# First feed-forward of a two-stream trunk layer: hidden products written to DRAM, then w2 as seven block products; x is read a second time

## The chip, the cores and the metric

The kernel runs on one core of one Trainium2 chip. The metric is device time in microseconds of one execution, the median of three runs. TensorE (PE) multiplies a stationary 128x128 block by up to 512 moving columns into PSUM; VectorE (DVE), ScalarE (ACT) and GpSimd (POOL) work elementwise; SyncE (SP) issues the transfers between DRAM and SBUF, in the order of its queue.

## The reference

One layer, 1024 latent tokens x and 256 context tokens, width 1024, hidden width 2816. Cut to what matters here:

```python
m_l = split(silu(c) @ ada_w + ada_b, 9)          # modulation, latents
m_c = split(silu(c_ctx) @ ada_w + ada_b, 9)      # modulation, context
x   = x   + 0.5 * m_l[2] * swiglu(modulate(rms_norm(x,   norm1_w), m_l[0], m_l[1]), w1, w3, w2)
ctx = ctx + 0.5 * m_c[2] * swiglu(modulate(rms_norm(ctx, norm1_w), m_c[0], m_c[1]), w1, w3, w2)
y   = token_mixing(modulate(rms_norm(x, norm2_w), m_l[3], m_l[4]),
                   modulate(rms_norm(ctx, norm2_w), m_c[3], m_c[4]), ...)
x   = x + m_l[5] * y
x   = x + 0.5 * m_l[8] * swiglu(modulate(rms_norm(x, norm3_w), m_l[6], m_l[7]), w1', w3', w2')
return rms_norm(x, final_norm_w)
# swiglu(h, w1, w3, w2) = (silu(h @ w1) * (h @ w3)) @ w2
```

## The kernel before

Everything is kept transposed: x is eight tiles (k) of 128 channels by 512 tokens for each of two latent token groups (tg 0 and 1), and eight of 128x256 for the context (tg 2). Each float32 operand is split into a high and a low part (`split`, L56: ScalarE copies the high part, VectorE or GpSimd subtracts for the low part), and one 128x128 block product is three matmuls (`mm3`, L61). The hidden width is 22 blocks f of 128, worked off in eleven pairs.

**Stage 1, first feed-forward of the latents.** `first1` (L632) and two calls of `classic` (L582) do three pairs plainly: for each block and each of w1 and w3, eight k for both token groups. From pair 3 on `sevens` (L599) multiplies the 2x2 arrangement (two halves of k by two token groups, two blocks f) with seven block products instead of eight (`seven`, L276; its weight sums in `seven_w`, L256). The sums of the activations T1 to T4 are made once ahead of it (`t12`, `t34_raw`, `t3_split`, `t4_split`, L493 to L526). In all pairs the product silu(h w1) * (h w3) stays in SBUF (`s3`, L545), and one pair later `Y` (L552) multiplies it plainly by w2 and adds it, gated, into x. So x stays in SBUF through the stage.

**Modulation.** Sixteen columns (shift and scale of the first norm) come early, in `first1`. 32 more latent columns follow at low priority in the plain pairs (`mod_col`, L100: a 512 KB load and a VectorE reduction over 1024 elements, into a ring of seven tiles). The context's 40 columns and 24 latent ones are made half by half during `sevens` (`mods_half`, L112: 256 KB loads through the ring `raw` that the weights use, MLATE = 17 per pair).

**Stage 2, context.** The context's x is loaded and normed, the last pair's `Y` of token group 1 runs, then `classic` and `Y` for the 256 context tokens, pair by pair; GpSimd makes the low parts of w1 and w3 there. The norm of group 1 is handed out over these pairs. Last come `Y` of the last pair for the context and for group 0, the norm of group 0, and a copy of x to DRAM (`xd`).

**Stage 3** is token mixing. **Stage 4**, the second feed-forward, is already in two phases: `hidden` (L397) makes all eleven pairs, nearly all with `chain` (L307, the seven products with accumulation in PSUM), and `g_out` (L357) writes seven activation sums of each pair to DRAM (`gd`). `w2_sums` (L375) writes four sums of w2's blocks per pair (`sd`). Then `back` (L404) does w2 as seven products, each over all eleven pairs, with `pair` loading one activation tile and one weight tile of 256 KB. Its last product also carries the final norm.

**Order.** Instructions are placed by a scheduler by priority: `high_priority(offset=WPRI)` moves weight loads and splits ahead, a negative offset moves work back. Each engine, and SP's queue, then runs its instructions in the fixed order. Rings that matter: `raw` 6 tiles, split weights 6, scratch `s` 7 tiles in the first feed-forward (NS) and 20 in the second.

## Time and profile before

| | us |
|---|---|
| three runs | 2242.12, 2242.82, 2245.99 |
| median | 2242.82 |
| the profiled execution's own time | 2242.13 |
| its span, first to last instruction | 2240.4 |

Roughly, by the windows view: the latents' first feed-forward runs to 720 us, the context to 950, mixing to 1570, the second feed-forward to the end. Of the kernel's 316.47 MB of transfers, 314.39 go through SP's queue.

How to read the rows. A row of a group has line, engine, operation, output <- input, shape and count, then busy time and the mean of one in ns, then the idle time of the engine just before, with what ended it. A row of windows has a stretch in us and, for each engine, busy us with the number of instructions in parentheses, then TensorE's granted clock, the busy share of the transfer engines and their GB/s. A row of waits has who waited for whom, the sum in us, how often, and the longest. A row of the timeline has start, duration, engine, line, operation. A row of one line's instructions has min/median/max of the duration in ns. SPq and POOLq are the queues of SyncE and GpSimd.

### The profile page before, as it was taken

What the parts mean: (1) busy time and instruction counts of PE and PEld (TensorE: products, weight loads), DVE (VectorE), ACT (ScalarE), POOL (GpSimd) and SP (SyncE); (2) the same over time, 40 slices, a digit from 0 to 9 for tenths busy, and PEclk for the clock granted to TensorE, in tenths of its full rate; (3) what the DMA queues carried; (4) which work ended last, traced back from release to release, by engine and by line L of the source; (5) the groups of instructions that cost most, each with busy time, mean ns of one, the idle gap of its engine ahead of it and who ended that gap; (6) DMA issues with size and microseconds to landing.
All of it is one profiled execution on the core that took longest, in us unless ns stands there. A gap on an engine that the chain in (4) does not pass through costs nothing. (4 is left out here: it accounts for less than half of the span.)

```text
span 2240.4 us, 32584 instructions
## 1 busy us (share of the span) xinstructions
PE 2148.4 (96%) x11598; PEld 1829.7 (82%) x11598; DVE 1590.9 (71%) x2901; ACT 919.1 (41%) x1681; POOL 291.4 (13%) x294
## 2 busy tenths in 40 slices
PE   4999999999999999999998999999999999999998
PEld 3888888888887999888877888778778888888888
DVE  7798888888888745763567446867776767675666
ACT  3323223232334554555653445334334343444553
POOL 2000000000002565431032112300000000010000
PEclk9999999999999999999999999999999999999999
DMA  7661444444434566463322223324135445467664
GB/s 246 215 234 40 123 136 137 132 132 136 132 104 136 152 184 186 151 179 107 100 66 73 78 77 88 103 74 164 59 123 166 165 149 170 145 202 239 200 198 151
DMA packets 175859, 316.47 MB, mean 141 GB/s; under 512 B 20880, under 2 KB 34128, under 8 KB 175696
## 3 DMA queue, kind: packets, MB, share of 16 engines
q1 hardware_dynamic: 175696, 314.39, 44.6%
q8 instruction: 91, 1.49, 0.3%
q14 instruction: 72, 0.59, 0.1%
HBM read 260.01 MB, written 45.91 MB: 137 GB/s over the span
## 5 line engine op out<-in xcount | busy, mean ns | idle before, releaser
L58 ACT ACTIVATE whi<-raw 128x512 fp32r<-128x512 f32 (+1 forms) x662 | 408.2, 623 | 805.3 <-PE psa L64 244.0
L59 DVE TENSOR_TENSOR wlo<-raw,whi 128x512 fp32r<-128x512 f32 (+1 forms) x544 | 377.5, 697 | 309.7 <-ACT whi L58 305.9
L63 PE MATMUL psa<-hh,whi 128*128 128x512 f32 (+1 forms) x1460 | 537.0, 369 | 7.7 <-ACT hh L195 7.7
L64 PE MATMUL psa<-hl,whi 128*128 128x512 f32 (+1 forms) x1460 | 537.8, 368 | 2.0 <-DVE hl L196 2.0
L65 PE MATMUL psa<-hh,wlo 128*128 128x512 f32 (+1 forms) x1460 | 537.1, 368 | 0.0
L63 PEld LDWEIGHTS psa<-hh,whi 128*128 128x128 f32 x1460 | 277.3, 190 | 50.9 <-ACT hh L195 9.1
L64 PEld LDWEIGHTS psa<-hl,whi 128*128 128x128 f32 x1460 | 277.8, 190 | 45.2 <-DVE hl L196 3.0
L65 PEld LDWEIGHTS psa<-hh,wlo 128*128 128x128 f32 x1460 | 277.7, 190 | 42.2
L59 POOL TENSOR_TENSOR wlo<-raw,whi 128x512 fp32r<-128x512 f32 (+1 forms) x118 | 158.9, 1362 | 760.5 <-ACT whi L58 753.4
L63 PE MATMUL psb<-ghi,whi 128*128 128x512 f32 (+1 forms) x528 | 188.2, 357 | 3.5 <-ACT ghi L58 2.1
L64 PE MATMUL psb<-glo,whi 128*128 128x512 f32 (+1 forms) x528 | 187.7, 356 | 0.7 <-DVE glo L59 0.6
L65 PE MATMUL psb<-ghi,wlo 128*128 128x512 f32 (+1 forms) x528 | 187.5, 355 | 0.0
L63 PE MATMUL psb<-hh,whi 128*128 128x512 f32 (+1 forms) x420 | 158.6, 380 | 2.3 <-ACT hh L195 1.8
L64 PE MATMUL psb<-hl,whi 128*128 128x512 f32 (+1 forms) x420 | 159.4, 379 | 1.5 <-DVE hl L196 1.5
L65 PE MATMUL psb<-hh,wlo 128*128 128x512 f32 (+1 forms) x420 | 159.1, 379 | 0.6 <-DVE wlo L59 0.6
L561 DVE SCALAR_TENSOR_TENSOR x<-psb,modl,x 128x512 f32<-128x512 f32 x176 | 128.6, 745 | 5.1 <-PE psb L65 4.9
L63 PEld LDWEIGHTS psb<-ghi,whi 128*128 128x128 f32 x528 | 100.2, 190 | 20.3 <-DVE x L561 2.8
L64 PEld LDWEIGHTS psb<-glo,whi 128*128 128x128 f32 x528 | 100.4, 190 | 14.5 <-DVE glo L59 1.1
L65 PEld LDWEIGHTS psb<-ghi,wlo 128*128 128x128 f32 x528 | 100.5, 190 | 13.7
L64 PE MATMUL psa<-wlo,hh 128*128 128x256 f32 (+1 forms) x320 | 94.7, 296 | 0.9 <-DVE wlo L59 0.9
L63 PE MATMUL psa<-whi,hh 128*128 128x256 f32 (+1 forms) x320 | 94.4, 295 | 0.2 <-ACT s L891 0.2
L63 PEld LDWEIGHTS psb<-hh,whi 128*128 128x128 f32 x420 | 79.6, 190 | 17.6 <-ACT hh L195 2.2
(370 smaller groups left out, 3750.1 us busy)
## 6 DMA issues: line engine op xcount, KB each, us to landing
raw<-in_w SPq DMA_DIRECT2D x385, 256.0 KB, 3.0
raw<-in_adaT SPq DMA_DIRECT2D x128, 256.0 KB, 3.2
gd<-s SPq DMA_DIRECT2D x77, 256.0 KB, 2.8
raw<-gd SPq DMA_DIRECT2D x77, 256.0 KB, 2.7
ada<-in_adaT SPq DMA_DIRECT2D x29, 512.0 KB, 4.7
s<-in_w SPq DMA_DIRECT2D x44, 256.0 KB, 4.8
sd<-s SPq DMA_DIRECT2D x44, 256.0 KB, 2.5
raw<-sd SPq DMA_DIRECT2D x44, 256.0 KB, 2.7
```

Source lines behind the costliest of these rows:

```text
L58: nc.scalar.activation(hi, src, AF.Copy)
L59: (eng or nc.vector).tensor_tensor(out=lo, in0=src, in1=hi.bitcast(F32), op=ALU.subtract)
L63: mm(ps, wa[0], xa[0], start=start, stop=False, skip_group_check=more)
L64: mm(ps, wa[0], xa[1], start=False, stop=False, skip_group_check=more)
L65: mm(ps, wa[1], xa[0], start=False, stop=stop, skip_group_check=more)
L561: nc.vector.scalar_tensor_tensor(out=x, in0=ps[:, :n], scalar=self.gates_m[int(tg == 2)][:, m:m + 1], in1=x, op0=ALU.mult, op1=ALU.add)
```

## The change

In the first feed-forward, `first1` and one further plain pair (`classic_g`) are followed by `hidden(4, ...)`, nine pairs of chains whose products go to DRAM; three modulation columns follow each chain. x's tiles are given up after the first norm and read again behind the hidden stage. `back` is taken apart into methods that both feed-forwards use: `back6` does six of the seven products. In the first feed-forward the seventh (product 4) runs behind the context, into PSUM tiles of its own. Only two of w2's four sums are stored (`sd` has two planes); the other two are made from two loads each when products 7 and 3 need them, through a ring of eight tiles (`raw2`) in the place of activations no longer needed. The context's norm runs inside `back6`, behind product 2, at an offset of -300 for its matmuls. Latent modulation columns of the groups 5, 7, 6 and 8 are made half by half in the context loop, six per pair. Columns that latents and context both need share one load. The scratch ring of the first feed-forward has 19 tiles.

```diff
-        self.gd = self.nc.dram_tensor("gd", (8, NP, P, 512), F32, kind="Internal").ap()
-        self.sd = self.nc.dram_tensor("sd", (8, NP, P, 512), F32, kind="Internal").ap()
+        self.gds = [self.nc.dram_tensor(f"gd{i}", (8, NP, P, 512), F32, kind="Internal").ap() for i in range(2)]
+        self.sds = [self.nc.dram_tensor(f"sd{i}", (2, NP, P, 512), F32, kind="Internal").ap() for i in range(2)]
...
-    def ada_tile(self, early):
+    def ada_tile(self):
-        i = self.ada % (AB if early else 4 + AB)
-        if i < AB:
-            return self.tile(self.dp, [P, D], F32, f"ada{i}")
-        return self.tile(self.f1w, [P, D], F32, f"w{i - AB + 1}")
+        return self.tile(self.dp, [P, D], F32, f"ada{self.ada % AB}")
...
+                m = self.mod[0][:, j:j + 1]
+                t = self.stile()
+                nc.sync.dma_start(t, self.I["adaT"][j][:, o:o + 512])
+                nc.vector.tensor_tensor_reduce(out=t, in0=t, in1=row, scale=1.0, scalar=m if o else self.col("ada_b")[:, j:j + 1],
...
+    def raw2(self, src):
+        self.nraw += 1
+        i = self.nraw % 8
+        t = self.tile(self.hp, [P, 512], F32, f"h{'hl'[i % 2]}0{4 + i // 2}")
+        self.nc.sync.dma_start(t, src)
+        return t
+
+    def w2_block(self, b, p):
+        o = 512 * (b // 10 - 1)
+        return self.w2[2 * p + b % 10 - 1][:, o:o + 512]
+
+    def w2_sums(self, p):
+        nc = self.nc
+        a21, a22, a11 = (self.stile() for _ in range(3))
+        for t, b in ((a21, 21), (a22, 22), (a11, 11)):
+            nc.sync.dma_start(t, self.w2_block(b, p))
+        nc.vector.tensor_tensor(out=a22, in0=a21, in1=a22, op=ALU.add)
+        nc.sync.dma_start(self.sd[0, p], a22)
+        nc.vector.tensor_tensor(out=a11, in0=a22, in1=a11, op=ALU.subtract)
+        nc.sync.dma_start(self.sd[1, p], a11)
+    def w2_tile(self, i, p):
+        block = lambda b: self.w2_block(b, p)
+        if i in (1, 2, 4):
+            return self.raw_half(block({1: 11, 2: 12, 4: 22}[i]))
+        if i in (5, 6):
+            return self.raw_half(self.sd[i - 5, p])
+        a, b = (self.raw2(x) for x in ((block(11), block(21)) if i == 7 else (block(12), self.sd[1, p])))
+        self.nc.vector.tensor_tensor(out=a, in0=a, in1=b, op=ALU.subtract)
+        return a
-    def hidden(self, f0):
+    def hidden(self, f0, mods=lambda: None):
         for f in range(f0, NF, 2):
             self.chain(self.w1, f, self.c_silu, self.psA)
-            self.w2_sums(f - 2)
+            mods()
+            self.w2_sums(f // 2 - 1)
             self.chain(self.w3, f, self.c_mul, self.psB)
-        self.w2_sums(NF - 2)
-
-    def back(self):
-        nc = self.nc
+            mods()
+        for p in [*range(f0 // 2 - 1), NP - 1]:
+            self.w2_sums(p)
+    def pair(self, i, p):
+        slots = [f"0{k}" for k in range(4)]
+        t = self.hslot(slots[self.nslot % 4])
+        self.nslot += 1
+        with self.tc.high_priority(offset=WPRI):
+            self.split(self.raw_half(self.gd[i, p]), *t)
+            return self.half(self.w2_tile(i, p)), t
...
+    def prod(self, i, ps, start):
+        for p in range(NP):
+            w, t = self.pair(i, p)
+            for m in range(4):
+                self.mms(ps[m], w, t, m, p, start)
...
+    def keep4(self, ps):
+        o = [self.stile() for _ in range(4)]
+        for m in range(4):
+            self.nc.scalar.copy(o[m], ps[m])
+        return o
+
+    def plus4(self, a, b):
+        for x, y in zip(a, b):
+            self.nc.vector.tensor_tensor(out=x, in0=y, in1=x, op=ALU.add)
+        return a
+
+    def add4(self, tg, q, src, o=0, e=512, ms=range(4)):
+        for m in ms:
+            x = self.x[tg][4 * q + m][:, o:e]
+            self.nc.vector.scalar_tensor_tensor(out=x, in0=src[m][:, o:e], scalar=self.gates_m[0][:, 4 * q + m:4 * q + m + 1],
+                                                in1=x, op0=ALU.mult, op1=ALU.add)
...
+    def back6(self, mid=lambda: None, keep=True):
+        A = self.bank4(self.psA)
+        self.prod(1, A, True)
+        c1 = self.keep4(A)
+        B = self.bank4(self.psB)
+        self.prod(2, B, True)
+        self.add4(0, 0, self.plus4(c1, B))
+        mid()
+        self.prod(6, A, False)
+        u2 = self.keep4(A)
+        B = self.bank4(self.psB)
+        self.prod(5, B, True)
+        c5 = self.keep4(B)
+        self.prod(7, A, False)
+        if keep:
+            u3 = self.keep4(A)
+            self.add4(1, 1, self.plus4(c5, u3))
+        else:
+            self.add4(1, 1, self.plus4(c5, A))
+            self.add4(0, 1, A)
+        self.prod(3, B, False)
+        self.add4(1, 0, self.plus4(u2, B))
+        return A
+
+    def back2(self):
...
+        A = self.back6()
...
-                w = hslot((slots[15:] + slots[:4])[p - 6]) if p >= 6 else tuple(self.tile(self.fp, [P, 512], F32R, "s", self.ns) for _ in "hl")
-                self.split(self.raw_half(self.w2_src(4, p)), *w)
+                w = self.hslot((slots[15:] + slots[:4])[p - 6]) if p >= 6 else tuple(self.tile(self.fp, [P, 512], F32R, "s", self.ns) for _ in "hl")
+                self.split(self.w2_tile(4, p), *w)
...
-        self.g[f, tg] = tuple(self.tile(self.fp, [P, 512], F32R, f"g{c}{min(tg, 1)}", 2)[:, :n] for c in ("hi", "lo"))
+        self.g[f, tg] = tuple(self.tile(self.gp, [P, n], F32R, "g" + c, 4) for c in ("hi", "lo"))
...
-    def sevens(self, f0, tp, extra=iter(())):
-        self.Y(f0 - 2, YORD)
+    def classic_g(self, f):
+        for i in range(2):
+            w = self.load_halves(self.w1[f + i])
+            for tg in LATTG:
+                self.c_silu(f + i, tg, self.H(w, tg), True)
+            w = self.load_halves(self.w3[f + i])
+            for tg in LATTG:
+                self.c_mul(f + i, tg, self.H(w, tg))
+
+    def t_make(self):
         self.t12()
         for k in range(4):
             t3, t4 = self.t34_raw(k)
             self.t3_split(k, t3)
             self.t4_split(k, t4)
...
-                        self.s1(f, tg, pss[tg][2 * f])
-                        self.s3(f, tg, pss[tg][2 * f + 1])
+                        self.c_silu(f, tg, pss[tg][2 * f], True)
+                        self.c_mul(f, tg, pss[tg][2 * f + 1])
...
+        self.first1(prep, ws)
+        cls("n1"), cls("f1w"), cls("xp")
+        self.tp = tp = opn("tp", "right")
+        dp2 = opn("dp2")
+        self.cs.append(self.cond_row("c_ctx", dp2))
+        todo = [(8 * m + k, ctxs) for m, ctxs in EMODS for k in range(KD)]
...
-        self.first1(prep, ws)
-        mods(MODS[0])
...
-        self.sevens(2 * CL, tp, self.mods_half(self.row, SMODS))
-        cls("dp2")
-        cls("tp")
+        self.t_alloc(tp)
+        self.classic_g(2)
+        self.t_make()
+        self.hidden(4, lambda: mods(MPER))
+        mods(len(todo))
+        cls("dp2"), cls("tp"), cls("dp")
+        xp = opn("xp", "right")
+        self.x = {}
+        self.load_x((xp, xp, None), (0, 1))
         hc = opn("hc", "right")
+        self.gp = hc
...
+        def ctx_in():
+            self.psN = self.psB
+            self.norm_mod(2, self.mcol(1, 1), self.mcol(0, 1), n2, LR1)
+
+        self.back6(ctx_in, False)
...
         pend = []
-        self.Y(NF - 2, [(1, 0, 512)], after)
+        after(1, 0, 512)
         CT = [(2, 0, 256)]
+        late = self.mods_half(hc, LMODS)
         for f in range(0, NF, 2):
             self.classic(f, (2,), mid=(lambda: self.Y(f - 2, CT)) if f else None, eng=[nc.gpsimd if e else None for e in CENG])
             for _ in range(NPEND if f else 0):
                 if pend:
                     pend.pop(0)()
-        self.Y(NF - 2, [(2, 0, 256), (0, 0, 512)], after)
+            for _ in range(6):
+                next(late, None)
+        self.Y(NF - 2, CT, after)
+        B = self.bank4(self.psB)
+        self.prod(4, B, True)
+        self.add4(0, 1, B)
+        after(0, 0, 512)
...
-        self.back()
+        self.back2()
...
-MLATE = 17
-SMODS = ((1, (1, 0, 2, 4, 3)), (0, (7, 6, 8)))
-EMODS = (2, 4, 3, 5)
+EMODS = ((2, (0, 1)), (1, (1,)), (0, (1,)), (4, (0, 1)), (3, (0, 1)))
+LMODS = (5, 7, 6, 8)
+MPER = 3
+LR1 = 300
 NH = 6
...
-NS = 7
+NS = 19
```

## The prediction

> **What bounds the kernel now.** I read the page's busy table first, then the windows view in steps of 40 us, then TensorE's waits by stage, then groups of instructions for durations.

> ```profile
> span 2240.4 us, 32584 instructions
> PE 2148.4 (96%) x11598; PEld 1829.7 (82%) x11598; DVE 1590.9 (71%) x2901; ACT 919.1 (41%) x1681; POOL 291.4 (13%) x294
> core 0: us, PE busy (x) PEld busy (x) DVE busy (x) ACT busy (x) POOL busy (x), PEclk, DMA share, GB/s
> 120.00:160.00 40.00, 40.00 (x178) 33.10 (x177) 39.23 (x65) 8.45 (x14) 0.00 (x0) 1.00 0.73 251
> 160.00:200.00 40.00, 40.00 (x178) 33.14 (x177) 39.61 (x64) 12.13 (x20) 0.00 (x0) 1.00 0.12 34
> ...
> 720.00:760.00 40.00, 35.07 (x272) 34.34 (x273) 36.95 (x56) 22.93 (x43) 20.56 (x14) 0.96 0.52 156
> ...
> 800.00:840.00 40.00, 40.00 (x335) 40.00 (x335) 19.55 (x37) 20.01 (x37) 25.94 (x21) 1.00 0.60 179
> ...
> 1720.00:1760.00 40.00, 40.00 (x178) 33.13 (x177) 26.56 (x42) 15.75 (x28) 0.00 (x0) 1.00 0.47 158
> ...
> 2000.00:2040.00 40.00, 40.00 (x178) 33.14 (x177) 26.04 (x41) 14.84 (x26) 7.72 (x8) 1.00 0.88 286
> ...
> 2080.00:2120.00 40.00, 40.00 (x178) 33.14 (x177) 23.86 (x41) 21.25 (x41) 0.00 (x0) 1.00 0.66 204
> ```

> The x beside PE counts matmuls. In the latent part of the first feed-forward (120 to 200 here) and in the whole second one (1720 to 2120) TensorE is busy 40.00 of 40.00 us, at full clock, with 178 matmuls of 512 columns: 40/178 = 0.2247 us each. That is a bound by count: one matmul less is 0.2247 us less, so long as nothing else starts to wait. In the context loop (800 to 840) it is 335 matmuls of 256 columns, 0.1194 us each. VectorE at 98 or 99% (39.23 and 39.61 of 40) did not take anything from TensorE there.

> **Matmuls removed.** A pair is two blocks f of 128 hidden columns; a plain matmul of one 128x128 block costs three instructions (mm3). Before, for latents: three plain pairs at 2 blocks x 2 matrices x 2 token groups x 8 k x 3 = 192; eight pairs of sevens at 2 matrices x 7 products x 4 k x 3 = 168; w2 for eleven pairs at 2 groups x 8 columns x 2 x 3 = 96. Sum 576 + 1344 + 1056 = 2976. After: two plain pairs, 384; nine pairs of chains, 1512; w2 as seven products x 11 pairs x 4 x 3 = 924. Sum 2820. The groups confirm the counts of before: 352 = 11 x 16 x 2, and 104 = 8 x 2 x 4 plus 40 of the second feed-forward.

> ```profile
> L63 PE MATMUL psb<-ghi,whi 128*128 128x512 f32 x352 | 137.7, 391 | 0.9 <-DVE x L561 0.6 <-DVE modc L134 0.2
> L63 PE MATMUL psa<-t1h,whi 128*128 128x512 f32 x104 | 40.5, 389 | 0.0
> ```

> 156 matmuls fewer x 0.2247 = **-35.1 us**. The context's own matmuls stay. The 391 ns in these rows overlap, so the pitch from the windows is the price, not the mean.

> **What the first hidden stage adds.** Its chains are the code of the second feed-forward's, which ran in 1720 to 1760 with VectorE busy 26.56 of 40, so 25.1 us in a pair's 168 x 0.2247 = 37.75 us. Two sums of w2 less per pair at 0.605 us (half of the 1.20 us between starts in the row below) leave 23.9. The modulation columns move here: 40 loads, 64 reductions, at six loads per pair.

> ```profile
> 79.25 1.29 DVE L59 TENSOR_TENSOR wlo<-raw,whi 128x512 fp32r<-128x512 f32 x2
> 80.45 0.69 DVE L59 TENSOR_TENSOR glo<-s,ghi 128x512 fp32r<-128x512 f32 x1
> L107 DVE CUSTOM_DVE_ANT_0 junk<-ada,condc,cols 128x1024 bf16<-128x1024 f32 x29 | 37.1, 1279 | 9.7 <-DMA ada<-in_adaT 9.5
> L122 DVE CUSTOM_DVE_ANT_0 raw<-raw,row,cols 128x512 f32<-128x512 f32 x64 | 46.7, 747 | 6.2 <-DMA raw<-in_adaT 5.8
> ```

> With 9.6 reductions per pair at 1.28 us that is 12.3, together 36.2 of 37.75 us, 96%. Three of the pairs get twelve reductions (15.4 us) and come to 39.3, 1.55 us over. I take 0, because the reductions are at low priority, their neighbours have room, and 98 to 99% was free in 120 to 200. If that cover is gone it costs 3 x 1.55 = 4.7 us.

> The sums T1 to T4 are made one pair earlier: 52 VectorE operations, 31.5 us at 0.605. They must fit beside one plain pair (192 x 0.2247 = 43 us), with some 27 other operations (8 left from the first pair, 8 splits and 8 products and sums of the plain one, and the first splits of the next), 16 us. That is 47.5 against 43, but T4 (8 operations) is needed only in the chain's seventh product, 16 us later. I take 0; without that slack it is 5 us. No modulation reductions stand there any more.

> **What the w2 phase adds.** Per pair and product two transfers of 256 KB against 12 x 0.2247 = 2.70 us, which 2080 to 2120 shows at 204 GB/s with TensorE full. Products 7 and 3 now load three, because the difference of two blocks is taken on the spot, in both feed-forwards: 3 x 262144 bytes / 2.70 us = 292 GB/s. From 2000 to 2040 the queues moved 286 with TensorE full, and the slowest ten microseconds in it were these:

> ```profile
> 2020.00:2030.00 10.00, 10.00 (x46) 8.29 (x45) 4.50 (x7) 3.46 (x6) 0.00 (x0) 1.00 0.86 266
> ```

> At a share of 0.86 that is not a ceiling: 266/0.86 is 309. I take 0. If 266 were the ceiling, a pair would take 2.96 instead of 2.70 us, 0.26 x 22 = 5.7 us in each feed-forward. VectorE does three operations per 2.70 us there (1.8 us). x comes in again as sixteen 256 KB loads while products 1 and 2 run; its first use is behind product 2, 22 x 2.70 = 59 us later, so nothing waits. In the second feed-forward, the last product's tiles for pairs 0 to 3 take over the places of the new ring, but the last of these is read about when product 4's loads start anyway, four pairs ahead of TensorE: 0.

> **What leaves the way into the context.** The context's norm stood between sevens and context; it now runs inside product 6, where VectorE has 16 of 40 us free. TensorE's waits in 690 to 800 were:

> ```profile
> PE psb L63 <- ACT ghi L58: 2.1, 1, 2.1
> PE psb L179 <- DVE ndiag L177: 1.6, 1, 1.6
> PE psa L64 <- DVE hl L196: 1.5, 1, 1.5
> PE psa L63 <- ACT hh L195: 1.2, 1, 1.2
> PE psa L179 <- DVE ndiag L177: 1.0, 1, 1.0
> PE psb L63 <- DVE x L561: 0.5, 1, 0.5
> ```

> The three on psa are that norm (its rows, then its high and low parts for the first context matmuls): **-3.7 us**. The other three (4.2 us) belong to the norm of the second token group and to a crowded VectorE, and stay; if they went too, -7.9.

> **What the context loop gets.** 64 half-width reductions, six per pair, come into a loop of 144 x 0.1194 = 17.2 us per pair. The queue of GpSimd does eight of the splits per pair there, VectorE four and two short ones:

> ```profile
> L59 POOL TENSOR_TENSOR wlo<-raw,whi x72: 1279/1296/1734, 759.1 to 914.5; 128x512 fp32r<-128x512 f32 x72
> L59 DVE TENSOR_TENSOR wlo<-raw,whi x36: 674/693/1346, 771.9 to 911.6; 128x512 fp32r<-128x512 f32 x36
> L59 DVE TENSOR_TENSOR glo<-s,ghi x18: 410/465/1220, 770.8 to 914.9; 128x256 fp32r<-128x256 f32 x18
> 33.43 1.27 DVE L107 CUSTOM_DVE_ANT_0 junk<-ada,condc,cols 128x1024 bf16<-128x1024 f32 x1
> 33.44 2.39 POOL L59 TENSOR_TENSOR w<-raw,w 128x512 fp32r<-128x512 f32 x1 [1.81 <-ACT w L58]
> ```

> In the last two rows a split on GpSimd that began just behind a reduction took 2.39 instead of 1.26 to 1.30 us: it stood for the reduction's length. So the two engines exclude each other for such instructions, and their times add: 8 x 1.296 + 4 x 0.693 + 2 x 0.465 = 14.1 us per pair, plus 6 x 0.747 = 4.5, is 18.6 against 17.2: 1.4 us over. Counted by the distance between starts (0.08 us less each on VectorE) it is 17.6, 0.4 over. Over 64/6 = 10.7 pairs that is 4 or 15 us, and 0 if the weights' buffers absorb it. I take **+4**, by the rows for distances. [...]

> Product 4, moved behind the context, is part of the 924. It gives 132 x 0.2247 = 29.7 us of work over the context's last norm where 48 matmuls stood: 0, or a gain of up to 2. The four extra additions into x run beside product 3.

> **Sum.** 2240.4 - 35.1 - 3.7 + 4 = 2205.6. The profiled execution took 2242.13 us (1.7 more than its span), and the median of the three runs is 2242.82, 2.4 above the span: **2208**.

> **Rivals.**
> - Context loop held by the lock at its full price, +15 instead of +4: 2219. For it: the row of 2.39. Against: GpSimd is idle 14 of 40 us in 800 to 840, and a wait there need not reach TensorE. 0.18.
> - Transfers bound products 7 and 3 in both feed-forwards, 2 x 5.7: 2219. For it the 266; against it the 286 over 40 us. 0.09.
> - VectorE bounds the hidden stage and the making of T, 4.7 + 5: 2218. Against it, 120 to 200. 0.09.
> - The whole 7.9 us at the entry goes and the lock costs nothing: 2240.4 - 35.1 - 7.9 + 2.4 = 2200. 0.10.
> - Slower than before: the queue of SP issues in order, and each of the 40 new loads of 512 KB takes one of only three buffers, so it stands at the queue's head until a low-priority reduction has freed one; behind it stand the weights. For it, SP did stand for VectorE, in 1700 to 2000:

> ```profile
> SPq L235 <- DVE wlo L59: 86.2, 48, 4.0
> ```

>  If each load held the weights up for one reduction beyond what the six buffers of weights cover, 40 x 1.28 = 51 us: 2259. It outweighs the gain from 0.87 us per load on (34.8/40). Against it, the same kind of load ran between the weights in 120 to 160 with TensorE full, though with seven buffers. 0.07.
> - The change doesn't do what it says: it would be so if TensorE's time there were not its matmul count, which 40.00 of 40.00 excludes; no chance of its own.

> **Numbers.** The forecast holds 0.47 with its own range of 2202 to 2214. Range: low is the gain of 2200 less the 2 us that product 4 may give, 2198; high is 2208 plus the lock's other 11, plus transfers at 11.4, 2230. That leaves out the slower rival and mixtures of several bounds. A measurement of this kernel can't tell changes under 0.2% (4.5 us). Faster by more than that takes all cases but the slower one and a part of its neighbourhood: 0.91; within 0.2%: 0.02; slower: 0.07.

> **What would show it.** PE instructions: 156 fewer in all. Windows of the first hidden stage and its w2 phase at 40.00 with x178, VectorE at 36 or more of 40 in the first seven chain pairs. No wait of TensorE on the context's norm rows. Context loop: fewer than 335 matmuls per 40 us, GpSimd's splits above 1.30 us on average, if the lock costs; 335 if not. Products 7 and 3 at some 290 GB/s and TensorE full. I am wrong if TensorE idles in the hidden stage behind whi or raw, with SP waiting on the reductions, or if the context loop stretches by more than 1.4 us a pair.

## The result and the profile after

The changed kernel takes **2278.14 us** (median of four runs, 2270.93 to 2280.38) against 2242.62 us for the kernel before, measured beside it. The ratio is 1.015 with a 95% interval of 1.0124 to 1.0175: slower by 35.5 us, where 34.8 us faster was forecast. The page of the profiled execution answers to the first lines of the page before:

```profile
span 2278.6 us, 32760 instructions
PE 2140.0 (94%) x11442; PEld 1820.4 (80%) x11442; DVE 1569.1 (69%) x2803; ACT 981.9 (43%) x1805; POOL 292.1 (13%) x294
```

TensorE executes 11442 matmuls instead of 11598: the 156 are gone as counted. Its busy time falls by 8.4 us instead of 35, because part of the rest ran at a lower clock (0.978 as the mean of the execution, 0.990 before), and the span grows by 38.2. So the work left, and waits and slow clock came. Spans and stages here are those of the profiled executions (2280.38 and 2242.13 us).

To find where, I cut the trace at the first and the last matmul of each stage (the stages differ in columns and count):

| stage | before, us | after, us | difference | expected from the count |
|---|---|---|---|---|
| first feed-forward up to the context | 685.2 | 656.7 | -28.5 | -53.9 (240 matmuls fewer x 0.2247) |
| context loop, 1584 matmuls of 256 columns | 205.0 | 253.2 | +48.2 | 0 |
| behind the context: 48, then 132 matmuls | 12.5 | 32.2 | +19.6 | +18.9 (84 x 0.2247) |
| all the rest, the second feed-forward in it | 1307.3 | 1306.1 | -1.1 | 0 |

The context loop costs 48 us more, and the first feed-forward keeps 25.4 us of what its count should have given.

**The context loop.** One row of the windows view for the loop of the kernel before and one for the kernel after (columns as in the prediction: PE, PEld, DVE, ACT, POOL busy with instructions, clock, share and speed of the queues):

```profile
718.00:920.00 202.00, 194.36 (x1579) 192.50 (x1579) 125.71 (x211) 103.47 (x193) 115.80 (x87) 0.98 0.58 174
```

```profile
690.00:940.00 250.00, 210.10 (x1577) 205.86 (x1576) 185.30 (x337) 104.63 (x197) 116.32 (x83) 0.92 0.66 214
```

The same number of matmuls takes 48 us longer. TensorE's idle time grew from 7.6 (202 - 194.36) to 39.9 us, which is 32; and at a mean clock of 0.92 instead of 0.98, (0.08 x 250) - (0.02 x 202) is another 16 (TensorE's busy time for the same work grew by 15.7, from 194.36 to 210.10). Both are needed to make 48: idle gaps do not only cost their own length here, slow stretches came with them (the clock records have eight at half rate in this loop, 41.0 us in all, against two of 3.41 us before). VectorE is nowhere near full (185 of 250), so this is not an engine out of time. TensorE's waits in the two halves of the loop, then those of SP and of VectorE in the whole of it:

```profile
PE psb L63 <- DVE x L541: 9.7, 2, 4.9
PE psb L64 <- DVE glo L59: 3.2, 2, 2.7
...
PE psb L64 <- DVE glo L59: 16.8, 6, 3.3
...
SPq L232 <- POOL wlo L59: 112.1, 65, 7.1
...
DVE s L119 <- DMA s<-in_adaT: 20.4, 11, 2.9
```

Of the kernel before, 690 to 940 us:

```profile
PE psb L64 <- DVE glo L59: 0.6, 1, 0.6
...
PE psb L63 <- DVE x L561: 0.5, 1, 0.5
...
SPq L235 <- POOL wlo L59: 131.6, 93, 10.3
```

TensorE waits for VectorE, for two short things: `glo`, the low part of a hidden tile, and the addition into x (L541) that frees a bank. VectorE executes in order, as the chain below shows (`glo` begins at 782.76, behind a reduction begun at 779.48 and a split begun at 781.10), and ahead of these stands a late modulation reduction (L119) which waits for its load. The load is late because SP issues in order too (760.09 and 774.84 below): a batch of six stands behind loads of weights (L232) that wait for GpSimd to free their buffers. SP waited for GpSimd before too, even longer; what is new is that loads which VectorE needs stand behind it. The timeline shows one such chain (start, length, engine, line, operation, and in brackets the idle time before it):

```profile
760.09 14.70 SPq L232 DMA_DIRECT2D raw<-in_w  x7
774.84 3.02 SPq L118 DMA_DIRECT2D s<-in_adaT  x6
...
779.33 2.96 POOL L59 TENSOR_TENSOR wlo<-raw,whi 128x512 fp32r<-128x512 f32 x2 [5.78 <-ACT whi L58]
779.48 1.69 DVE L119 CUSTOM_DVE_ANT_0 s<-s,row,cols 128x512 f32<-128x512 f32 x1 [1.80 <-DMA s<-in_adaT]
...
781.10 1.74 DVE L59 TENSOR_TENSOR wlo<-raw,whi 128x512 fp32r<-128x512 f32 x1
782.76 0.41 DVE L59 TENSOR_TENSOR glo<-s,ghi 128x256 fp32r<-128x256 f32 x1
...
783.09 0.74 DVE L119 CUSTOM_DVE_ANT_0 s<-s,row,cols 128x512 f32<-128x512 f32 x1
...
783.23 0.58 PE L64 MATMUL psb<-glo,whi 128*128 128x256 f32 x1 [2.66 <-DVE glo L59]
```

Seven loads of weights take 14.70 us to issue; only then come the six for the reductions. At 779.48 a reduction begins, 1.80 us late for its load, beside a split on GpSimd; it takes 1.69 us. Behind it one of VectorE's own splits takes 1.74, again beside GpSimd (the median of such a split in the prediction's row is 0.693), and `glo` stands behind both. At 783.09 the next one, with GpSimd quiet, takes 0.74. TensorE gets its `glo` 2.66 us late. So three theories stand for the 48 us. **A**: the loads are late and bunched, and VectorE stands in order for them. **B**: reductions and GpSimd's splits shut each other out, which lengthens both. **C**: the loads hold up the weights in SP's queue.

**The first feed-forward.** Three places there lost matmuls. Four rows of windows, with 44.5 matmuls to 10 us at full clock:

```profile
140.00:180.00 40.00, 34.26 (x132) 26.20 (x131) 37.47 (x64) 17.14 (x30) 0.00 (x0) 0.91 0.49 164
200.00:330.00 130.00, 130.00 (x574) 107.23 (x573) 123.59 (x205) 52.26 (x92) 0.00 (x0) 1.00 0.66 214
510.00:540.00 30.00, 21.85 (x87) 17.29 (x86) 14.02 (x24) 14.51 (x28) 0.00 (x0) 0.89 0.94 317
580.00:620.00 40.00, 36.08 (x151) 29.41 (x150) 21.61 (x43) 19.51 (x38) 0.69 (x1) 0.91 0.46 146
```

In 140 to 180 us 46 matmuls are missing of 178 (10.3 us), in 510 to 540 46 of 133 (10.4), in 580 to 620 27 of 178 (6.1; the kernel before missed 5 here). That is 25.7 us net, about all of the 25.4. The last place is the context's norm, where TensorE stands for the diagonal of its rows:

```profile
PE psb L176 <- DVE ndiag L174: 3.4, 1, 3.4
```

Between the three the hidden stage is full (200 to 330: 130.00 of 130), with VectorE at 95%.

The middle one is the reload of x, which the timeline shows in SP's queue:

```profile
511.37 4.15 SPq L642 DMA_DIRECT2D x<-in_xT  x8
515.73 0.53 SPq L232 DMA_DIRECT2D raw<-gd  x1
517.33 2.27 SPq L642 DMA_DIRECT2D x<-in_xT  x4
520.01 0.33 SPq L232 DMA_DIRECT2D raw<-in_w  x1
520.67 3.68 SPq L642 DMA_DIRECT2D x<-in_ctxT  x6
522.07 0.63 ACT L58 ACTIVATE hh<-raw 128x512 fp32r<-128x512 f32 x1 [8.70 <-DMA raw<-gd]
...
526.14 0.79 PE L63 MATMUL psb<-hh,whi 128*128 128x512 f32 x1 [7.22 <-ACT whi L58]
```

Eighteen loads of x and the context are issued around two loads that TensorE needs; ScalarE waits 8.70 us for one of these, TensorE 7.22.

### The profile page after: what moved, and what is told of

Same layout as the page of the kernel before. It is cut to its first block, busy times and chain, and to the rows that moved or that the text cites. A ratio compares the mean times of both kernels' runs of the same rounds, so it can differ in the third digit from the quotient of the medians.

```text
span 2278.6 us, 32760 instructions
## 1 busy us (share of the span) xinstructions
PE 2140.0 (94%) x11442; PEld 1820.4 (80%) x11442; DVE 1569.1 (69%) x2803; ACT 981.9 (43%) x1805; POOL 292.1 (13%) x294
## 5 line engine op out<-in xcount | busy, mean ns | idle before, releaser
L58 ACT ACTIVATE whi<-raw 128x512 fp32r<-128x512 f32 (+1 forms) x657 | 405.6, 623 | 775.8 <-issue 234.9
L59 DVE TENSOR_TENSOR wlo<-raw,whi 128x512 fp32r<-128x512 f32 (+1 forms) x539 | 381.1, 710 | 330.7 <-ACT whi L58 325.3
L63 PE MATMUL psa<-hh,whi 128*128 128x512 f32 (+1 forms) x1416 | 521.2, 369 | 5.7 <-ACT hh L192 5.7
L64 PE MATMUL psa<-hl,whi 128*128 128x512 f32 (+1 forms) x1416 | 521.6, 368 | 0.5 <-DVE hl L193 0.5
L63 PEld LDWEIGHTS psa<-hh,whi 128*128 128x128 f32 x1416 | 270.3, 191 | 46.6 <-ACT hh L192 6.4
L64 PEld LDWEIGHTS psa<-hl,whi 128*128 128x128 f32 x1416 | 270.5, 191 | 41.6 <-DVE hl L193 1.2
L63 PE MATMUL psb<-hh,whi 128*128 128x512 f32 (+1 forms) x740 | 285.7, 387 | 11.6 <-ACT whi L58 9.7
L64 PE MATMUL psb<-hl,whi 128*128 128x512 f32 (+1 forms) x740 | 285.8, 386 | 0.3 <-DVE hl L59 0.3
L65 PE MATMUL psb<-hh,wlo 128*128 128x512 f32 (+1 forms) x740 | 284.9, 386 | 1.1 <-DVE wlo L59 1.1
L59 POOL TENSOR_TENSOR wlo<-raw,whi 128x512 fp32r<-128x512 f32 (+1 forms) x118 | 162.9, 1398 | 232.6 <-ACT whi L58 223.2
L63 PEld LDWEIGHTS psb<-hh,whi 128*128 128x128 f32 x740 | 140.5, 190 | 41.7 <-ACT whi L58 11.4
L65 PEld LDWEIGHTS psb<-hh,wlo 128*128 128x128 f32 x740 | 140.5, 190 | 29.6 <-DVE wlo L59 2.1
L64 PEld LDWEIGHTS psb<-hl,whi 128*128 128x128 f32 x740 | 140.7, 190 | 28.3 <-DVE hl L59 1.1
L59 DVE TENSOR_TENSOR hl<-raw,hh 128x512 fp32r<-128x512 f32 x159 | 110.7, 702 | 21.6 <-ACT hh L58 21.0
L58 ACT ACTIVATE hh<-raw 128x512 fp32r<-128x512 f32 x159 | 97.2, 620 | 29.4 <-DMA raw<-gd 24.5
L64 PE MATMUL psa<-wlo,hh 128*128 128x256 f32 (+1 forms) x320 | 94.6, 296 | 2.1 <-DVE wlo L59 2.1
L63 PE MATMUL psa<-whi,hh 128*128 128x256 f32 (+1 forms) x320 | 94.4, 295 | 0.2 <-ACT s L867 0.2
L65 PE MATMUL psa<-whi,hl 128*128 128x256 f32 (+1 forms) x320 | 93.6, 293 | 0.0
L64 PE MATMUL psb<-glo,whi 128*128 128x256 f32 x176 | 56.7, 322 | 20.1 <-DVE glo L59 20.0
```

What stands on the lines that cost most here:

```text
L58: nc.scalar.activation(hi, src, AF.Copy)
L59: (eng or nc.vector).tensor_tensor(out=lo, in0=src, in1=hi.bitcast(F32), op=ALU.subtract)
L63: mm(ps, wa[0], xa[0], start=start, stop=False, skip_group_check=more)
L64: mm(ps, wa[0], xa[1], start=False, stop=False, skip_group_check=more)
L65: mm(ps, wa[1], xa[0], start=False, stop=stop, skip_group_check=more)
```

## The experiments

All edits are against the changed kernel, unless a run says otherwise. "Loop" is the context loop's time, "first part" that of the first feed-forward up to the context, both cut as in the table above and read from the one profiled execution of each run. What such a reading is worth: the seven runs whose loop has no late work (1 and 7 to 12) have loops of 205.3 to 207.6 us, and runs with the same code up to the context (the changed kernel, 1, 2, 3 and 6) have first parts of 654.7 to about 657.5. Differences of 2 or 3 us between two runs show nothing.

**1. No late columns.** The 64 late loads and reductions are left out; a constant stands in their place, so the columns of groups 5 to 8 are not computed.

```
-        late = self.mods_half(hc, LMODS)
+        nc.vector.memset(self.mod[0][:, 40:72], 0.3)
...
-            for _ in range(6):
-                next(late, None)
```

> Leaves out the 64 late half-width modulation loads and reductions of the context loop (modulation groups 5 to 8 are set to 0.3 instead). Every theory: the context loop shrinks from 253 us towards the 205 us of before, because no wait of TensorE on x or glo is left; 2228 to 2240 us. If the loop stays above 235 us, the loss is not in the late modulation at all.

Measured: 2231.58 us, ratio to the kernel before 0.9958 (0.994 to 0.9976). Loop 205.3, first part 654.7. The late columns are the whole of the loop's 48 us: without them it is as before. Rows of this run, with which 8 to 10 are compared:

```profile
140.00:180.00 40.00, 33.15 (x127) 25.33 (x126) 37.11 (x63) 16.62 (x30) 0.00 (x0) 0.91 0.49 158
...
500.00:550.00 50.00, 43.72 (x184) 35.66 (x184) 26.42 (x43) 23.70 (x44) 0.00 (x0) 0.93 0.94 313
550.00:580.00 30.00, 30.00 (x134) 24.86 (x133) 19.12 (x31) 11.84 (x21) 0.00 (x0) 1.00 0.87 287
580.00:620.00 40.00, 35.88 (x156) 29.38 (x155) 23.54 (x46) 20.58 (x41) 0.70 (x1) 0.96 0.48 152
```

**2. Loads alone.** The reductions are left out, the 64 loads stay.

```
-                nc.vector.tensor_tensor_reduce(out=t, in0=t, in1=row, ...
+        nc.vector.memset(self.mod[0][:, 40:72], 0.3)
```

> Keeps the 64 loads, leaves the 64 reductions out (groups 5 to 8 set to 0.3). Theory A (the loads are issued late and in bunches of six, and VectorE stands in order for them): nobody waits for them now, so within 6 us of the kernel without late modulation. Theory B (lock between VectorE's reductions and GpSimd's splits): the same. Theory C (the six loads hold up the weights behind them in SP's queue): over 15 us slower than the kernel without late modulation.

Measured: 2237.31 us, ratio 0.9988 (0.9969 to 1.0007). Loop 212.5: the transfers and their places in SP's queue (theory C) cost 7.2 us (5.7 by the medians of the whole kernel). C as the main cause, over 15 us, falls.

**3. Reductions alone.** The loads are left out, and each reduction takes the row twice; the late columns are sums of other data.

```
-                nc.sync.dma_start(t, self.I["adaT"][j][:, o:o + 512])
-                nc.vector.tensor_tensor_reduce(out=t, in0=t, in1=row, ...
+                nc.vector.tensor_tensor_reduce(out=t, in0=row, in1=row, ...
```

> Keeps 64 reductions of the same size, in the same places, on a tile that is already there (row by row; groups 5 to 8 get other values), and leaves the 64 loads out. Theory A: within 8 us of the kernel without late modulation. Theory B: the loop stays long, 15 us or more above the kernel without late modulation, with GpSimd's splits and the reductions lengthened by each other. Theory C: as A.

Measured: 2259.28 us, ratio 1.0077 (1.0048 to 1.0107). Loop 234.1, 28.8 us more than without (27.7 by the medians), with no load to wait for. Theory A as the only cause falls. What ran in the loop (mean ns of one behind the comma):

```profile
L118 DVE CUSTOM_DVE_ANT_0 s<-row,modl 128x512 f32<-128x512 f32 x32 | 33.1, 1062 | 3.4 <-ACT row L114 3.4
L118 DVE CUSTOM_DVE_ANT_0 s<-row,cols 128x512 f32<-128x512 f32 x32 | 30.2, 966 | 0.0
```

A reduction takes 966 or 1062 ns on average, where the kernel before had 747. The mean hides two kinds: by their starts and ends 28 of the 64 overlap a split on GpSimd and take 1364 ns on average, the other 36 take 752 at most. That speaks for B, but a VectorE that is busy 63 us more could also do it by order alone.

**4. Loads earlier.** The loads of a batch are written down one pair ahead of its reductions.

```
+            ready, held = held, self.mods_load(late.pop(0)) if late else []
...
+            for x in ready:
+                self.mods_reduce(row, *x)
```

> The same work as after, but each iteration's loads are issued one pair earlier than their reductions (batches of 7 or 6). Theory A: most of the context loop's loss goes, loop 210 to 222 us, 2238 to 2250 us in all. Theory B: no change against after, 2265 to 2282. Theory C: no change either.

Measured: 2276.63 us, ratio 1.0155 (1.0125 to 1.0184), loop 246.4. This run does not tell A from B: the planner moved the reductions up again, close behind the loads (nine of the 64 even ahead of the loop), and VectorE still stood for them:

```profile
DVE s L125 <- DMA s<-in_adaT: 13.4, 7, 3.2
```

**5. One input, first try.** Reductions alone as in 3 (its line is the one removed), each a plain sum over the row with one input.

```
-                nc.vector.tensor_tensor_reduce(out=t, in0=row, in1=row, ...
+                nc.vector.tensor_reduce(out=m, in_=row, op=ALU.add, axis=mybir.AxisListType.X)
```

> Left out: the 64 late loads, and each late reduction multiplies nothing: it is a plain sum over the row (one input from SBUF instead of two), so the late modulation columns are not computed. Same place, same count, same order as in the run with reductions alone, whose context loop took 234.1 us (205.3 without them). Theory B (a reduction with two SBUF inputs and GpSimd's splits shut each other out for their whole length): with one input the shutting out is gone, a reduction's mean in the loop stays at its undisturbed length and below 0.9 us, and the loop takes 206 to 214 us. Rival (plain VectorE time and order: 64 instructions of 0.6 to 0.75 us ahead of the splits): the loop stays at 228 to 234 us.

Measured: 2237.0 us, ratio 0.9968 (0.9956 to 0.9981), loop 208.5, inside theory B's bounds, but for a wrong reason. The groups view for the whole kernel shows where the sums ran (least, middle and greatest ns, then first and last start):

```profile
L118 DVE TENSOR_REDUCE modl<-row x64: 668/676/684, 569.6 to 692.1; 128x1 f32<-128x512 f32 x64
```

They ran before the loop, all but the last four: they write into no tile of the ring, so nothing held them back (in run 6, where they do, they stay in the loop). The run says only that 43 us of VectorE's time cost little in 569 to 692 us.

**6. One input, in place.** The same sum, written into a tile of the ring (again against 3).

```
-                nc.vector.tensor_tensor_reduce(out=t, in0=row, in1=row, ...
+                nc.vector.tensor_reduce(out=t[:, 0:1], in_=row, op=ALU.add, axis=mybir.AxisListType.X)
```

> Left out: the 64 late loads; each late reduction is a plain sum over the row with one input from SBUF, so the late modulation columns are not computed. Unlike the first try, it writes into a tile of the same ring as the reductions, so it keeps their place in the context loop: six per pair. The first try showed 0.671 us for one such sum, against 0.747 for an undisturbed reduction with two inputs. Theory B (shutting out between two-input reductions and GpSimd's splits): a sum stays near 0.67 us with splits running beside it, GpSimd's splits stay near 1.35 us, and the loop is 206 to 214 us, against 234.1 with the two-input reductions. Rival (plain VectorE time and order): 26 us of the 28.8 stay, the loop is 228 to 234 us.

Measured: 2239.58 us, ratio 0.9991 (0.9979 to 1.0002). Loop 215.7.

```profile
L59 POOL TENSOR_TENSOR wlo<-raw,whi 128x512 fp32r<-128x512 f32 x86 | 115.2, 1358 | 98.1 <-ACT whi L58 94.8 <-PE psa L64 2.1 <-DVE s L118 0.4
L118 DVE TENSOR_REDUCE s<-row 128x1 f32<-128x512 f32 x64 | 41.6, 675 | 3.6 <-ACT row L114 3.6
```

All 64 are in the loop. 34 of them overlap a split on GpSimd and take 674 ns on average, the other 30 take 675; in the first try, where 3 of 64 overlapped one, the median was 676. With one input no sum was lengthened (686 ns at most). The same row for GpSimd has a mean of 1465 ns in run 3, 1358 here and 1385 in run 1. The loop sits 10.4 us above the one without late columns (8.0 by the medians), 1.7 above what theory B gave, and 18.4 below the one with two inputs. So of the 28.8 us, some 10.4 is VectorE's time and order, and 18.4 goes with the second input; some of the 18.4 (64 x 0.07 = 4.6 us of VectorE's time) is the plain difference in length. The sum also writes one column instead of 512 and is another operation; that this does not matter is argued from the overlaps in run 3, no run shows it alone. Runs 3 and 6 side by side: beside a split 1364 ns against 752 at most with two inputs, 674 against 675 with one.

**7. Late columns in the hidden stage.** The whole computation, with the late columns as full-width low-priority columns behind the 40 that stand there.

```
-EMODS = ((2, (0, 1)), ..., (3, (0, 1)))
-MPER = 3
+EMODS = ((2, (0, 1)), ..., (3, (0, 1)), (5, (0,)), (7, (0,)), (6, (0,)), (8, (0,)))
+MPER = 4
```

> The late columns (groups 5, 7, 6, 8) are made in the hidden stage, as 32 more full-width low-priority columns behind the 40 that stand there, four per chain instead of three; the context loop has none. There VectorE was busy 26 of 40 us from 320 to 480 us, 54 us free in all, GpSimd does nothing, and 32 x 1.28 us is 41 us. Theory (A and B alike: it is the place beside GpSimd's splits that costs): the context loop returns to 205 us, the hidden stage stays full, and the kernel takes about 2231 us, as the run without the late columns. Rival (the columns cost what they cost wherever they stand, VectorE fills up): TensorE idles in the hidden stage and the gain is under half of the 47 us, so 2255 us or more.

Measured: **2230.56 us**, ratio to the kernel before 0.9944 (0.9932 to 0.9957). Loop 206.7. The stretch that took them in:

```profile
330.00:480.00 150.00, 148.87 (x653) 121.87 (x652) 126.68 (x207) 59.70 (x105) 0.00 (x0) 1.00 0.71 235
```

VectorE rises to 84% there and TensorE loses 1.1 us (the first part as a whole takes 659.6, 2.9 more than in the changed kernel). It is the place and not the work that cost 48 us: the whole computation is 47.6 us faster than the changed kernel.

**8. x one tile per pair** (on run 1: the late columns left out). A one-column copy from a pair's weights holds each load of x.

```
+            if self.xq:
+                tg, k = self.xq.pop(0)
+                self.load_x(self.xpools, (tg,), (k,), w[0][:, 0:1].bitcast(F32))
...
+                if gate is not None:
+                    nc.gpsimd.tensor_copy(t[:, 0:1], gate)
```

> On the kernel without the late columns (they are left out again, 2231.6 us; first feed-forward to the context 654.7 us): the 24 loads of x and of the context are no longer issued in one row but one per pair, each held by a one-column copy from that pair's weights. Theory D (the row of loads ahead of the weights in SP's queue stops TensorE for 7.2 us at 520 and halves its clock after): the wait is gone, 654.7 becomes 643 to 648. Rival (the bytes bind, not their order): 653 to 656, with the waits spread over products 1 and 2.

Measured: 2228.65 us, ratio 0.994 (0.9923 to 0.9956); first part 660.5, against 654.7 in run 1. The windows and TensorE's wait in 575 to 625 us:

```profile
500.00:550.00 50.00, 47.31 (x202) 37.49 (x202) 25.34 (x42) 22.53 (x44) 10.62 (x15) 1.00 0.86 272
...
580.00:620.00 40.00, 30.51 (x123) 24.04 (x122) 18.83 (x38) 17.43 (x34) 0.69 (x1) 0.87 0.48 155
```

```profile
PE psb L176 <- DVE ndiag L174: 8.1, 1, 8.1
```

In the stretch of the reload run 1 had 184 matmuls, this one 202 and full clock: theory D holds for that stretch, 4 us, though 20 of the 222 that fit are still missing. But the next places took it back: 550 to 580 holds 114 instead of 134, the wait at the context norm grew from 3.7 to 8.1 us, and 580 to 620 holds 123 instead of 156 (138 to 156 in the runs whose code there is the same). The expected 643 to 648 did not come. How much was lost in all is open: the profiled executions took 2235.16 us here and 2228.05 in run 1, where the medians are 2228.65 and 2231.58.

**9. T before the modulation columns** (on run 1). The first modulation tiles are held until T4's last split.

```
+        if self.gate:
+            nc.gpsimd.tensor_copy(t[:, 0:1], self.gate.pop())
...
+        self.gate = [self.T[3][3][1][:, 0:1].bitcast(F32)] * AB
```

> On the kernel without the late columns (left out again): the first three modulation tiles of the hidden stage are held until the last of T4 is split, so no low-priority reduction runs on VectorE before T3 and T4 are made. Theory E (eight reductions at 127 to 135 us delay T3 and T4, and TensorE idles 6.9 us in 140 to 180 us, with the clock at 0.91): the stretch 140 to 180 is full, 654.7 becomes 646 to 650. Rival (T3 and T4 wait for something else, the plain pair's own work or buffers): 653 to 656, 140 to 180 as before.

Measured: 2229.67 us, ratio 0.9939 (0.9925 to 0.9953); first part 651.9, 2.8 us less. 

```profile
140.00:180.00 40.00, 34.74 (x148) 26.99 (x147) 37.01 (x62) 18.25 (x32) 1.37 (x3) 1.00 0.46 149
```

148 matmuls instead of 127 in run 1, at full clock, but 30 are still missing. Run 1 is the lowest of the nine runs with this stretch unchanged, which hold 127 to 144, 134 on average; runs 11 and 12, with the same edit, hold 149 and 148. So the reductions explain about 3 us of the stretch (14 x 0.2247); the rest stays when they are gone. VectorE is at 93% there with the making of T and the chain's own splits, which is the reading I take for the rest; no run took T's own work away.

**10. The context norm's rows later** (on run 1). They stand five pairs behind the column sums, neither at low priority.

```
+            r = self.rstd_col(self.squares(self.x[2], CTX, n2), CTX, n2)
+            yield
+            pr = self.rstd_rows(r, CTX, n2)
...
+            if mid and p == 5:
+                next(mid)
```

> On the kernel without the late columns (left out again; 2231.6 us, first feed-forward to the context 654.7 us): the context norm's row matmuls are written down five pairs behind its column sums, inside product 6, and no longer at low priority. Theory F (TensorE reaches the rows 4 us before the diagonal is there, and the second row matmul comes 10 us behind the first while ScalarE stands in order for it): the waits of 3.7 us and of ScalarE's 10 us go, 580 to 620 us holds 170 matmuls or more instead of 157, 654.7 becomes 648 to 652. Rival (the place does not matter, the chain of four engines is as long anywhere): 653 to 656 and a wait of 3 us or more on the diagonal.

Measured: 2226.24 us, ratio 0.9924 (0.9909 to 0.9939); first part 652.2, 0.2 above what theory F gave.

```profile
550.00:580.00 30.00, 27.52 (x119) 22.42 (x118) 20.48 (x36) 11.30 (x20) 0.98 (x1) 0.94 0.86 278
580.00:620.00 40.00, 40.00 (x179) 33.10 (x178) 26.35 (x48) 22.56 (x42) 0.00 (x0) 1.00 0.65 204
```

The stretch of the norm is full now (179), 23 matmuls better than run 1. But 550 to 580, full before (134), misses 15. Of runs 8 to 10 this is the only one whose interval lies clear of run 1's (0.9909 to 0.9939 against 0.994 to 0.9976), and only just.

**11 and 12. All four edits, whole computation.** Run 11 joins 7 to 10. In run 12 the column sums alone go back to low priority.

> The whole computation, with four edits together: late columns in the hidden stage, modulation tiles held until T4 is made, x and context loaded one tile per pair, the context norm's rows behind five pairs of product 6. If the losses add up as the single runs show them (2230.6 with the late columns moved; 4.5 us in 140 to 180 from the held tiles, 4.5 us in 500 to 550 from the spread loads, 3 to 7 us from the norm): 2214 to 2220 us. Rival (what is gained in one place is lost in the next one, as the spread loads did: 500 to 550 us gained 4.5 us and the norm's wait grew from 3.7 to 8.1): 2226 to 2232 us.

> The whole computation, the four edits of the run before together (2227.1 us), with one thing put back: the context norm's column sums are at low priority again, its rows stay behind five pairs of product 6. In the run before TensorE stood 5.9 us at the column sums for VectorE's last addition behind product 2, and 550 to 580 us held 100 matmuls instead of 133. Theory F (both waits come from where the norm's small matmuls stand in TensorE's order): the 5.9 us go and no other wait over 2 us takes their place between 550 and 620 us, the first feed-forward's part falls from 649.2 to 640 to 645 us, and the kernel to 2217 to 2223 us. Rival (the norm's chain costs TensorE one wait wherever it stands): a wait of 3 us or more on nacc, nr or ndiag there, and 2225 to 2230 us.

Measured: run 11 **2227.1 us**, ratio 0.9932 (0.9918 to 0.9945), loop 207.5, first part 649.2. Run 12 2228.86 us, ratio 0.9944 (0.9928 to 0.996), loop 207.4, first part 656.0. TensorE's waits at the norm, first of run 11, then of run 12:

```profile
PE psb L166 <- DVE s L412: 5.9, 1, 5.9
```

```profile
PE psb L178 <- DVE ndiag L176: 6.9, 1, 6.9
```

Both times the rival's range was met (2226 to 2232, and 2225 to 2230). Taking a wait of the norm away from one place put one of 6 to 7 us at another: at the sums (the bank that they need is freed by VectorE's last addition) or at the rows. Of the gains of 8, 9 and 10 little adds up (the intervals of 7, 11 and 12 overlap); moving the late columns is nearly all of the distance from 2278 to 2227. Run 7 is the simplest version that is faster than both kernels.

## Why the prediction was wrong

- **156 matmuls, -35.1: right** as a count and as a price where TensorE is full. The first part is 240 matmuls shorter, the stretch behind the context 84 longer and 19.6 us (18.9 by the count).
- **The context loop, +4: the step that failed.** It was argued as a sum of engine times, "18.6 against 17.2", and bounded at +15. The lock, a split on GpSimd that stands for a reduction on VectorE, was seen in the row of 2.39 us, but the measured term is 48.2: 44 of the 73 us between the forecast's -34.8 and the span's +38.2. A sum of times bounds an engine's throughput; this loop was not near it (VectorE 185 of 250 us). The sum looked at GpSimd ("a wait there need not reach TensorE"); the waits came by VectorE, 33.3 of TensorE's 39.9 us. What the loop pays for is order: a `glo` or an addition that TensorE needs at once stands behind reductions that nobody needs soon. The runs give 7.2 us for the loads alone, 10.4 for VectorE's time and order, 18.4 for the second input, each good to 2 or 3 us. With loads and reductions both there it is 47.9, so some 11.9 us come only then; the trace names VectorE's 20.4 us of standing for late loads as the likely place, but no run isolates it, since run 4 did not delay the reductions as meant.
- **What the sum left out was the clock.** About 16 of the 48 us are matmuls at a lower granted clock after idle gaps (0.92 in the loop, 0.98 before). A wait priced at its own length is priced too low here.
- **"x comes in again ... so nothing waits": wrong.** x itself was early enough; the loads of weights issued behind it were not. The argument looked at the first use of x and not at what stands behind x in SP's queue. 10.4 us in that stretch; run 8 shows 4 of them to be the order of the loads.
- **Reductions at low priority cost 0, T costs 0 (bound 5): wrong in one stretch.** The hidden stage did stay full with VectorE at 95%, as predicted. But in 140 to 180 us 10.3 us went, twice the bound. "No modulation reductions stand there any more" did not hold: reductions that were ready slipped in ahead of T3 and T4, which VectorE made from 140 to 162 us; seven of them between these two rows of the timeline, both included:

```profile
123.60 1.28 DVE L104 CUSTOM_DVE_ANT_0 junk<-ada,condc_ctx,cols 128x1024 bf16<-128x1024 f32 x1
...
134.17 1.28 DVE L104 CUSTOM_DVE_ANT_0 junk<-ada,condc_ctx,cols 128x1024 bf16<-128x1024 f32 x1
```

  Low priority orders what is ready together, it does not hold back what is ready first. By run 9 such reductions account for about 3 us; the cause of the rest is open.
- **The context's norm, -3.7 for its waits at the entry: those went, and came back elsewhere.** The waits on psa are gone from the loop's entry. "It now runs inside product 6, where VectorE has 16 of 40 us free" took free time for cover; TensorE waited there for `ndiag` all the same, 6.1 us with the clock, and runs 10 to 12 mostly moved the wait.
- **Products 7 and 3, 0: right.** The windows from the end of product 5 on:

```profile
620.00:660.00 40.00, 40.00 (x178) 33.12 (x177) 27.30 (x44) 20.11 (x37) 0.00 (x0) 1.00 0.86 276
660.00:690.00 30.00, 30.00 (x143) 25.00 (x142) 25.18 (x39) 11.63 (x21) 9.71 (x7) 1.00 0.68 229
```

  TensorE is full in both, with the queues at up to 276 GB/s; the predicted need was 292. **Second feed-forward, 0: right** (-1.1 for everything behind, which differs by up to 7.5 us between runs that share its code).
- **The slower rival** had the right sign and part of the mechanism (SP's queue in order, loads that stand for reductions), but at the wrong place: in the hidden stage, with its 40 columns, nothing idled. The late 64 half-columns in the context loop did it, and there the chance given to any loss beyond 15 us was none. That its 2259 is the forecast nearest to 2278 is luck. "If the context loop stretches by more than 1.4 us a pair" was the right test: it stretched by 48.2 / 10.7 = 4.5.

## What to carry to other kernels

Price background work by what stands behind it on each in-order queue it enters (VectorE, SP, TensorE itself for a small matmul), not by the sum of engine times: 185 busy us of 250 cost 48 here, while 127 of 150 in another stage cost 1 to 3. Put it where no GpSimd instruction runs beside it (reductions with two inputs took 1364 ns on average beside GpSimd's splits in run 3, 752 at most without) and nothing urgent follows on its engine; the same columns moved from the context loop to the hidden stage were worth 47.6 us with no other edit. And work that is merely at low priority runs whenever it is ready (seven reductions from 123.60 to 134.17 us ahead of T3 and T4 here): if it must not run early, it needs a dependency, and a removed wait has to be looked for again at the next place before it is counted as a gain.

## What the runs showed of the hardware

In this execution waits of TensorE came with stretches at a lower clock. In 520 to 530 us, with the wait of 7.22 us, the granted clock was 0.68 and 9 matmuls ran:

```profile
520.00:530.00 10.00, 3.86 (x9) 3.08 (x10) 4.15 (x9) 6.50 (x15) 0.00 (x0) 0.68 1.01 342
```
